# Four accumulating PSUM banks as four tensors of 512 columns instead of two of 1024, with a feature evicted in two halves

## The chip, the core and the metric

The kernel runs on one core of one Trainium2 chip. The metric is the device time of one execution in microseconds; the number given for a kernel is the median over its runs. In the profile, PE is the engine that multiplies matrices (PEld its weight loads, which run beside the multiplications), DVE the vector engine, ACT the scalar engine, POOL the general engine and SP the one that mostly issues transfers. Matmuls write to PSUM, a memory of eight banks here, each of which holds 512 fp32 columns on 128 partitions. A matmul of this kernel writes at most one bank; DVE and ACT read the finished sums from there ("evict" them) into SBUF.

## The reference

One layer of a conditioned decoder over 1024 positions and 1024 channels, in fp32. Cut to what matters:

```
mod = silu(c) @ ada_w + ada_b;  shift, scale, gate = split(mod, 3)
h = rms_norm(x, norm_w) * (1 + scale) + shift
hq, hf, hi, hz, gq, gk, gv, gz, ga, mg = split(h @ w_in)        # one wide projection
# hgrn: 8 heads of 128, gated linear recurrence
f = lb + (1 - lb) * sigmoid(hf);  k = (1 - lb) * sigmoid(-hf)
y_h = rms_norm(chunked_gated_linear_attention(silu(hq), k, hi, log f), hgrn_norm_w) * silu(hz)
# gla: 4 heads, key 128, value 256
log_a = log_sigmoid(ga @ alpha_w + alpha_b) / 16
y_g = rms_norm(chunked_gated_linear_attention(gq, gk, gv, log_a), gla_norm_w) * silu(gz)
merged = sigmoid(mg_0) * (y_h @ w_branch_0) + sigmoid(mg_1) * (y_g @ w_branch_1)
out = rms_norm(x + gate * (merged @ w_out), final_norm_w)
```

## The kernel before

Every large product is made of matmuls of 128 x 128 weights by 128 x 512 columns. To keep fp32 accuracy each operand is split into a high and a low part (ACT casts, L211 and its like; DVE subtracts, L212 and its like), and each product takes three matmuls.

The program has these stages. The **start** loads and normalises x and forms h. The **first group** (L386) makes six half rows of features in six accumulators `accs`: four PSUM banks and the two halves of `sc_ps`; DVE evicts them at L362 and L364 (`qk_out`). Then **V stage 0** (`Vstage`, matmuls at L1879, evictions at L1762, L1764, L1782, L1786 and L1790) makes values by a Strassen-like scheme: seven products in the order 1, 2, 5, 3, 6, 7, 4, each into the same four banks with 12 matmuls to a bank, six for one pair of operands and six for the next, and each bank evicted before the next product may start on it. The **features** (`mm_feat`, L594) are 34 blocks of 128 channels by 1024 positions, each 48 matmuls into two banks: 8 for silu(gz) and 24 for the hgrn part, of which 16 are evicted by a sigmoid on ACT (L949) and a product on DVE (L950), as the 8 of gz are too; 8 by two sigmoids (L1079, L1080); and two of gla_k by a DVE copy. V stage 1 stands among them. Beside them run twelve attention heads (L626 to L823), whose small matmuls (L652, L683, L741, L798, L817, L819) are slipped in between and write to `sc_ps` and to the `pm` tiles. The **last stages** (L1330) form the branch products and the gates in a ring of banks, four of which are the accumulating banks, lent at L1941, and the **out stage** (L1507) makes the output.

PSUM has three pools: `ps_d` holds the four accumulating banks as two tensors of 128 x 1024, two banks each (names pd...); `ps_s` holds one tensor `sc_ps` of two banks; `ps_m` two tensors of one bank (pm...). `dtile()` takes a tensor from `ps_d`; where single banks are wanted, the code cuts it in halves, so a matmul still writes one bank:

```
acc0 = [dtile(), dtile()]
accs = [acc0[f // 2][:, (f % 2) * 512:(f % 2) * 512 + 512] for f in range(4)]
```

Beyond the start, whose order is written out by hand, a scheduler decides at compile time which instruction stands where in each engine's queue, and which semaphores an instruction waits for. Evictions carry a raised priority. Each engine then runs its own queue in that fixed order.

Of the kernel before, what the change touches and what calls it, by code (L numbers as in the profile page):

```python
# [10 lines left out]
F32 = mybir.dt.float32  # L11
F32R = mybir.dt.float32r
I32 = mybir.dt.int32
AF = mybir.ActivationFunctionType
ALU = mybir.AluOpType

P = 128
D = 1024
T = 1024
# [70 lines left out]
def hybrid_trunk_kernel(  # L90
# [6 lines left out]
    nc = tc.nc  # L97
# [3 lines left out]
    cp = ctx.enter_context(tc.tile_pool(name="const", bufs=1))  # L101
    sp = ctx.enter_context(tc.tile_pool(name="slots", bufs=1))
    dp = ctx.enter_context(tc.tile_pool(name="dram", bufs=1, space=bass.MemoryType.DRAM))
    ps_d = ctx.enter_context(tc.tile_pool(name="ps_d", bufs=2, space=bass.MemoryType.PSUM))
    ps_s = ctx.enter_context(tc.tile_pool(name="ps_s", bufs=1, space=bass.MemoryType.PSUM))
    ps_m = ctx.enter_context(tc.tile_pool(name="ps_m", bufs=2, space=bass.MemoryType.PSUM))
    S = Slots(sp, N_SLOTS)
# [1 line left out]
    cnt = [0]  # L109

    def dtile():
        cnt[0] += 1
        return ps_d.tile([P, T], F32, tag="d", name=f"pd{cnt[0]}")

    def mtile():
        cnt[0] += 1
# [251 lines left out]
    def make_ga(half):  # L368
# [8 lines left out]
        if half == 0:  # L377
            S.free(*[hT[half, i] for i in range(4)])

    acc0 = [dtile(), dtile()]  # L380
    accs = [acc0[f // 2][:, (f % 2) * 512:(f % 2) * 512 + 512] for f in range(4)]
    accs += [sc_ps[:, 0:512], sc_ps[:, 512:1024]]

    def product(half, d, f, n):
# [202 lines left out]
    def mm_feat(wt, rhs, ps, w=P):  # L587
        hi, lo = wt
        for k in range(KT):
            n = 0  # L590
            r_hi, r_lo = rhs(k)
            for a, b in ((hi, r_hi), (hi, r_lo), (lo, r_hi)):
                for th in range(2):
                    nc.tensor.matmul(ps[0:w, th * 512:(th + 1) * 512], a[:, k, 0:w],  # L594
                                     b[:, th * 512:(th + 1) * 512],
                                     start=(k == 0 and n == 0), stop=(k == KT - 1 and n == 2))
                n += 1
            yield

    class Feat:  # L600
# [15 lines left out]
        def run(self):  # L616
            ps = dtile()
            yield from mm_feat(self.wt, self.rhs, ps, self.w)
            S.free(*self.wt)
            self.done(ps)  # L620
# [325 lines left out]
    def silu_done(store, key):  # L946
        def f(ps):
            s = S.get([T])
            nc.scalar.activation(s, ps, AF.Sigmoid)  # L949
            nc.vector.tensor_mul(s, s, ps)  # L950
            store[key] = s
        return f

# [59 lines left out]
    def gla_k_done(h):  # L1013
        def f(ps):
            t = S.get([T])
            nc.vector.tensor_copy(t, ps)
            if h == 3:
                nc.gpsimd.dma_start(k3_d, t)
                S.free(t, sent=True)
            else:  # L1020
                g_state[("k", h)] = t
        return f
# [53 lines left out]
    def hf_done(h):  # L1076
        def fn(ps):
            f, k = S.get([T]), S.get([T])
            nc.scalar.activation(f, ps, AF.Sigmoid)  # L1079
            nc.scalar.activation(k, ps, AF.Sigmoid, scale=-1.0)  # L1080
            nc.vector.tensor_scalar(f, f, oml[:, h:h + 1], lb[:, h:h + 1], ALU.mult, ALU.add)
            nc.vector.tensor_scalar_max(f, f, F_FLOOR)
            nc.vector.tensor_scalar_mul(k, k, oml[:, h:h + 1])
            h_state[("f", h)] = f
            h_state[("k", h)] = k
        return fn
# [205 lines left out]
    R = Banks()  # L1292
# [83 lines left out]
    def last_stages():  # L1376
        for n, (b, p) in enumerate(GROUPS):
            for i in range(4):
                if i % 2 == 0:
                    ahead(2 * n + i // 2, 4, 2)  # L1380
                pairs[b, i].run(p)
                pairs[b, i].after(p)
                for f in at.get((b, p, i), ()):
                    f()
            if b:
                for z in H.pop((0 if b == 1 else b, p)):
                    S.free(*z)
# [277 lines left out]
    for b in (2, 3):  # L1665
        for p, i, z in ((3, 3, "11"), (6, 1, "21"), (6, 3, "12"), (7, 2, "22")):
            after(b - 1, p, i, lambda b=b, z=z: load_quad(b, z))
            if b == 3:
                p, i = {(3, 3): (7, 2), (6, 1): (7, 3), (6, 3): (4, 2), (7, 2): (4, 3)}[p, i]
# [77 lines left out]
    class Vstage:  # L1747
# [5 lines left out]
            self.snap = {}  # L1753

        def start(self):
            pair = [dtile() for _ in range(2)]
            self.bank = [pair[i // 2][:, i % 2 * 512:i % 2 * 512 + 512] for i in range(4)]

        def take(self, i, scale=1.0):
            t = Q.get()  # L1760
# [178 lines left out]
    stream.go()  # L1939
    S.free(*h_hi, *h_lo)  # L1940
    lent = [dtile() for _ in range(2)]  # L1941
    R.lend([pd[:, i * 512:i * 512 + 512] for pd in lent[::-1] for i in range(2)])
    last_stages()
    out_stage()

# [28 lines left out]
```

## Time and profile before

| | |
|---|---|
| three runs | 1201.57, 1200.64, 1201.26 us; median 1201.26 |
| the profiled execution | 1201.55 us, of which the span of the trace is 1199.8 |
| PE matmuls | 1170.1 us busy, 98% of the span |
| DVE | 846.3 us busy, 71% |
| ACT | 584.9 us busy, 49% |
| POOL | 124.3 us busy, 10% |
| mean granted PE clock | 0.998 |

A matmul's busy time overlaps that of the one behind it, so that PE's busy share says how much of the span some matmul was in flight, not that it stepped at its full rate. The idle time before a group of instructions is listed with the instruction whose end let it go on ("<-", the releaser); it is the place to look for what a busy engine loses.

### The profile page before, as it was taken

The page shows a single profiled execution, that of the slowest core. Times are in us where ns is not written, and L with a number is a line of the kernel's source. Part 1 is how long each engine was busy: PE and PEld are TensorE (multiplying, and loading weights), DVE is VectorE, ACT ScalarE, POOL GpSimd, SP SyncE. Part 2 cuts the span into 40 slices and gives each one's busy share as a digit, 9 for nine tenths or more (in the row PEclk, how much of TensorE's full clock was granted, in tenths as well). Part 3 has the DMA queues.
Part 4 walks back from the last instruction along what each step waited for, and adds up shares of the span by engine and source line. Part 5 has one row for each costly group of instructions (what it writes and reads, how often), then busy time and mean ns, then how long its engine had stood idle before and what let it go on. Part 6 is the DMA issues. An engine that isn't in the chain of part 4 may idle for free.

```text
span 1199.8 us, 20303 instructions
## 1 busy us (share of the span) xinstructions
PE 1170.1 (98%) x8137; PEld 951.0 (79%) x8137; DVE 846.3 (71%) x1270; ACT 584.9 (49%) x860; POOL 124.3 (10%) x257
## 2 busy tenths in 40 slices
PE   7999999999999999999999999999999999999997
PEld 6776777888878688888888878778888888878886
DVE  4745667657664955887897798695553866988994
ACT  5674462673455445334433435456643644444554
POOL 4111111000110211111111010001120000000000
PEclk9999999999999999999999999999999999999999
DMA  9745445155474855665565454255688846335523
GB/s 324 262 173 201 150 161 176 52 178 175 167 273 141 296 195 161 209 210 160 173 197 178 130 203 124 78 169 179 225 312 284 285 152 210 125 108 173 171 99 134
DMA packets 150641, 221.24 MB, mean 184 GB/s; under 512 B 8971, under 2 KB 107329, under 8 KB 150546
## 3 DMA queue, kind: packets, MB, share of 16 engines
q1 hardware_dynamic: 132114, 158.37, 42.4%
q0 software_dynamic: 18384, 61.56, 13.3%
q8 instruction: 64, 1.05, 0.4%
q14 instruction: 31, 0.25, 0.1%
q10 hardware_dynamic: 48, 0.01, 0.0%
HBM read 154.37 MB, written 65.54 MB: 183 GB/s over the span
## 4 chain that ended last, share of the span: by engine, by line
PE 65%; issue 20%; DVE 6%; ACT 4%; DMA 3%; POOL 2%; SPq 0%; POOLq 0%; DVEq 0%; ACTq 0%
PE pd L594 16%; PE pd L1330 11%; PE pd L1879 9%; PE sc_ps L1330 6%; PE pm L1330 6%; PE pd L1507 3%; PE pd L386 2%; PE sc_ps L1507 2%; PE pm L1507 1%; PE pm L798 1%; POOL ws L1182 1%; DVE b L212 1%; PE pm L817 1%; DMA b<-in_ada_w_dram 1%; PE sc_ps L386 1%
## 5 line engine op out<-in xcount | busy, mean ns | idle before, releaser
L594 PE MATMUL pd<-b,b 128*128 128x512 f32 x1632 | 393.8, 396 | 0.2 <-ACT b L1762 0.2
L594 PEld LDWEIGHTS pd<-b,b 128*128 128x128 f32 x1632 | 303.0, 189 | 65.8 <-issue 0.7
L1330 PE MATMUL pd<-b,b 128*128 128x512 f32 x720 | 173.2, 392 | 0.6 <-DVE b L1422 0.4
L1879 PE MATMUL pd<-b,b 128*128 128x512 f32 x672 | 162.7, 396 | 7.1 <-DVE b L1790 3.4
L1330 PEld LDWEIGHTS pd<-b,b 128*128 128x128 f32 x720 | 133.9, 188 | 31.2 <-DVE b L1422 0.9
L1879 PEld LDWEIGHTS pd<-b,b 128*128 128x128 f32 x672 | 123.4, 188 | 40.7 <-ACT b L1762 4.0
L212 DVE TENSOR_TENSOR b<-b,b 128x1024 fp32r<-128x1024 f32 x78 | 94.2, 1222 | 48.4 <-ACT b L211 48.1
L1273 DVE TENSOR_TENSOR b<-b,b 128x1024 fp32r<-128x1024 f32 x56 | 68.2, 1221 | 69.2 <-ACT b L1272 53.0
L1272 ACT CAST b<-b 128x1024 fp32r<-128x1024 f32 x56 | 58.4, 1050 | 65.0 <-PE pm L1330 18.1
L211 ACT CAST b<-b 128x1024 fp32r<-128x1024 f32 x78 | 79.8, 1047 | 6.4 <-PE pd L1879 3.0
L1330 PE MATMUL sc_ps<-b,b 128*128 128x512 f32 x324 | 78.7, 391 | 0.4 <-ACT b L1302 0.4
L1330 PE MATMUL pm<-b,b 128*128 128x512 f32 x300 | 72.1, 389 | 0.0
L1330 PEld LDWEIGHTS sc_ps<-b,b 128*128 128x128 f32 x324 | 60.4, 188 | 13.9 <-ACT b L1302 1.1
L1249 ACT CAST b<-b 128x1024 fp32r<-128x1024 f32 x48 | 49.7, 1050 | 43.9 <-PE pd L1330 15.9
L1250 DVE TENSOR_TENSOR b<-b,b 128x1024 fp32r<-128x1024 f32 x48 | 57.7, 1219 | 18.4 <-ACT b L1249 12.2
L1330 PEld LDWEIGHTS pm<-b,b 128*128 128x128 f32 x300 | 56.3, 188 | 11.7
L203 DVE TENSOR_TENSOR b<-b,b 128x1024 fp32r<-128x1024 f32 (+1 forms) x36 | 35.1, 983 | 29.5 <-ACT b L202 29.4
L386 PE MATMUL pd<-b,b 128*128 128x512 f32 x192 | 52.3, 405 | 2.8 <-DVE b L362 1.9
L1182 POOL DMA_DIRECT2D ws<-b x64 | 34.9, 546 | 193.6 <-DVE b L1174 107.4
L703 ACT COPY xb<-b 128x512 f32<-128x512 f32 x48 | 29.7, 621 | 50.8 <-PE sc_ps L683 23.8
L817 PE MATMUL pm<-scT,b 128*128 128x128 f32 x256 | 46.9, 275 | 0.0
L386 PEld LDWEIGHTS pd<-b,b 128*128 128x128 f32 x192 | 34.4, 188 | 15.4 <-DVE b L362 2.9
(317 smaller groups left out, 1699.6 us busy)
## 6 DMA issues: line engine op xcount, KB each, us to landing
b<-in_w_in_dram SPq DMA_DIRECT2D x72, 512.0 KB, 4.3
ws<-b POOLq DMA_DIRECT2D x64, 256.0 KB, 3.9
b<-ws SPq DMA_DIRECT2D x32, 512.0 KB, 4.4
b<-in_x_dram SPq DMA_DIRECT2D x16, 512.0 KB, 4.4
b<-in_ada_w_dram SPq DMA_DIRECT2D x32, 256.0 KB, 6.5
v<-b POOLq DMA_DIRECT2D x32, 256.0 KB, 3.7
b<-v SPq DMA_DIRECT2D x16, 512.0 KB, 5.2
b<-fx SPq DMA_DIRECT2D x16, 512.0 KB, 4.5
```

What stands on the lines that cost most here:

```text
L211: held(nc.scalar.copy(hi, src))
L212: nc.vector.tensor_sub(lo, src, hi.bitcast(F32))
L386: nc.tensor.matmul(accs[f], wg(a, d, f), b[d][:, half * 512:half * 512 + 512], start=(d == 0 and n == 0), stop=(d == KT - 1 and n == 2))
L594: nc.tensor.matmul(ps[0:w, th * 512:(th + 1) * 512], a[:, k, 0:w], b[:, th * 512:(th + 1) * 512], start=(k == 0 and n == 0), stop=(k == KT ...
L817: nc.tensor.matmul(o, vch(ch)[:, vh * P:(vh + 1) * P], scT[:, ch, :], start=True, stop=(ch == 0))
L1249: nc.scalar.copy(hi, src)
L1250: nc.vector.tensor_sub(lo, src, hi.bitcast(F32))
L1272: nc.scalar.copy(hi, t)
L1273: nc.vector.tensor_sub(lo, t, hi.bitcast(F32))
L1330: nc.tensor.matmul(o, a[:, sl], c, start=(p in (1, 5) and kt == 0 and n == 0), stop=(kt == 3 and n == 2), skip_group_check=True)
L1507: nc.tensor.matmul(o, a, b, start=(p in (1, 5) and kt == 0 and n == 0), stop=(kt == 3 and n == 2), skip_group_check=True)
L1879: nc.tensor.matmul(st.bank[i], x_, w_, start=(p in (1, 5) and kk == 0 and a == 0 and n == 0), stop=(kk == 1 and a == 1 and n == 2), skip_g ...
```

## The change

`ps_d` now holds four tensors of 128 x 512, one bank each, and `dtile()` returns a list of two of them. The banks, and which matmul adds to which sum, are the same as before; `accs`, the banks of `Vstage` and those lent to the last stages are now four tensors. An instruction that reads or writes 1024 columns of a feature at once can no longer do so, since they lie in two tensors: the sigmoid and product of `silu_done`, the two sigmoids of `hf_done` and the copy of `gla_k_done` are each done for 512 columns and then for the other 512.

```diff
-    ps_d = ctx.enter_context(tc.tile_pool(name="ps_d", bufs=2, space=bass.MemoryType.PSUM))
+    ps_d = ctx.enter_context(tc.tile_pool(name="ps_d", bufs=4, space=bass.MemoryType.PSUM))
...
     def dtile():
         cnt[0] += 1
-        return ps_d.tile([P, T], F32, tag="d", name=f"pd{cnt[0]}")
+        return [ps_d.tile([P, 512], F32, tag="d", name=f"pd{cnt[0]}_{i}") for i in range(2)]
...
-    acc0 = [dtile(), dtile()]
-    accs = [acc0[f // 2][:, (f % 2) * 512:(f % 2) * 512 + 512] for f in range(4)]
+    accs = dtile() + dtile()
     accs += [sc_ps[:, 0:512], sc_ps[:, 512:1024]]
...
                 for th in range(2):
-                    nc.tensor.matmul(ps[0:w, th * 512:(th + 1) * 512], a[:, k, 0:w],
+                    nc.tensor.matmul(ps[th][0:w, :], a[:, k, 0:w],
...
     def silu_done(store, key):
         def f(ps):
             s = S.get([T])
-            nc.scalar.activation(s, ps, AF.Sigmoid)
-            nc.vector.tensor_mul(s, s, ps)
+            for th in range(2):
+                sl = slice(th * 512, th * 512 + 512)
+                nc.scalar.activation(s[:, sl], ps[th], AF.Sigmoid)
+                nc.vector.tensor_mul(s[:, sl], s[:, sl], ps[th])
             store[key] = s
...
             t = S.get([T])
-            nc.vector.tensor_copy(t, ps)
+            for th in range(2):
+                nc.vector.tensor_copy(t[:, th * 512:th * 512 + 512], ps[th])
...
             f, k = S.get([T]), S.get([T])
-            nc.scalar.activation(f, ps, AF.Sigmoid)
-            nc.scalar.activation(k, ps, AF.Sigmoid, scale=-1.0)
+            for th in range(2):
+                sl = slice(th * 512, th * 512 + 512)
+                nc.scalar.activation(f[:, sl], ps[th], AF.Sigmoid)
+                nc.scalar.activation(k[:, sl], ps[th], AF.Sigmoid, scale=-1.0)
...
         def start(self):
-            pair = [dtile() for _ in range(2)]
-            self.bank = [pair[i // 2][:, i % 2 * 512:i % 2 * 512 + 512] for i in range(4)]
+            self.bank = dtile() + dtile()
...
     lent = [dtile() for _ in range(2)]
-    R.lend([pd[:, i * 512:i * 512 + 512] for pd in lent[::-1] for i in range(2)])
+    R.lend([pd for pds in lent[::-1] for pd in pds])
```

The scheduler puts instructions in another order on PE and DVE. Line numbers behind the first edit shift by up to four: L386 becomes L385, L645 becomes L644, L1790 becomes L1793, L1879 becomes L1882.

PE at the end of the first group, before: the three matmuls that finish the first half of `sc_ps`, then three that finish the second bank of pd_173. The first banks of pd_173 and pd_174 are finished ahead of these rows.

```order
L386 MATMUL sc_ps<-b_146,b_168 128x512
L386 MATMUL sc_ps<-b_154,b_168 128x512
L386 MATMUL sc_ps<-b_146,b_170 128x512
L386 MATMUL pd_173<-b_146,b_162 128x512
L386 MATMUL pd_173<-b_154,b_162 128x512
L386 MATMUL pd_173<-b_146,b_166 128x512
```

The same place in the changed kernel (pd_1_176 is the fourth bank, pd_0_1139 and pd_1_1140 the first two of V stage 0, which take the room of the first two accumulators).

```order
L385 MATMUL pd_1_176<-b_154,b_162 128x512
L385 MATMUL pd_1_176<-b_146,b_166 128x512
L385 MATMUL sc_ps<-b_146,b_168 128x512
L385 MATMUL sc_ps<-b_154,b_168 128x512
L385 MATMUL sc_ps<-b_146,b_170 128x512
L1882 MATMUL pd_0_1139<-b_1078,b_139 128x512
L1882 MATMUL pd_0_1139<-b_1079,b_139 128x512
L1882 MATMUL pd_0_1139<-b_1078,b_147 128x512
L1882 MATMUL pd_0_1139<-b_1078,b_140 128x512
L1882 MATMUL pd_0_1139<-b_1079,b_140 128x512
L1882 MATMUL pd_0_1139<-b_1078,b_148 128x512
L1882 MATMUL pd_1_1140<-b_1078,b_139 128x512
```

All four banks are now finished in the order first, second, third, fourth ahead of the first half of `sc_ps`, and V stage 0 begins straight behind it; before, six matmuls of the group (banks two and four) stood behind that place.

PE in V stage 0 at the end of product 7, before: the last three of five matmuls into the third bank (in pd_1138), and then the first three of the six into the second bank, which lies in pd_1137; the six into the first bank, in pd_1137 too, stand ahead of all of these. b_1499 and b_1500 are the weights, b_1505 and b_1506 the columns.

```order
L1879 MATMUL pd_1138<-b_1499,b_1506 128x512
L1879 MATMUL pd_1138<-b_1499,b_1505 128x512
L1879 MATMUL pd_1138<-b_1500,b_1505 128x512
L1879 MATMUL pd_1137<-b_1499,b_1505 128x512
L1879 MATMUL pd_1137<-b_1500,b_1505 128x512
L1879 MATMUL pd_1137<-b_1499,b_1506 128x512
```

The same place in the changed kernel: the last two of the first bank and the first three of the second.

```order
L1882 MATMUL pd_0_1139<-b_1504,b_1509 128x512
L1882 MATMUL pd_0_1139<-b_1503,b_1510 128x512
L1882 MATMUL pd_1_1140<-b_1503,b_1509 128x512
L1882 MATMUL pd_1_1140<-b_1504,b_1509 128x512
L1882 MATMUL pd_1_1140<-b_1503,b_1510 128x512
```

Behind these rows stand three more of the second bank, six matmuls of pd_0_1141 and six of pd_1_1142, and only then the first of product 4 on pd_0_1139; before, product 4's first three on the first bank stood ahead of product 7's six on the fourth. The second bank now follows the first without a piece of the third between them, and so it is through both V stages: six matmuls to each bank in turn.

DVE at the evictions of product 7 (L1790), beside the preparation of a head (L645 to L648, L654 to L657) and a split (L212), before:

```order
L212 TENSOR_TENSOR b_1586<-b_1318,b_1585 128x1024
L1790 TENSOR_TENSOR b_1327<-pd_1137,b_1327 128x512
L645 TENSOR_TENSOR xb<-b_1519,b_863 128x32x8
L646 TENSOR_TENSOR xb<-b_1519,b_863 128x32x8x2
L212 TENSOR_TENSOR b_1623<-b_1517,b_1622 128x1024
L1790 TENSOR_TENSOR b_1327<-pd_1137,b_1327 128x512
L1790 TENSOR_TENSOR b_1350<-pd_1138,b_1350 128x512
L647 TENSOR_TENSOR xb<-xb,b_863 128x32x16
```

The same place in the changed kernel:

```order
L212 TENSOR_TENSOR b_1590<-b_1322,b_1589 128x1024
L1793 TENSOR_TENSOR b_1331<-pd_0_1139,b_1331 128x512
L1793 TENSOR_TENSOR b_1331<-pd_1_1140,b_1331 128x512
L644 TENSOR_TENSOR xb<-b_1523,b_865 128x32x8
L645 TENSOR_TENSOR xb<-b_1523,b_865 128x32x8x2
L1793 TENSOR_TENSOR b_1354<-pd_0_1141,b_1354 128x512
L646 TENSOR_TENSOR xb<-xb,b_865 128x32x16
L1793 TENSOR_TENSOR b_1354<-pd_1_1142,b_1354 128x512
L647 TENSOR_TENSOR xb<-xb,b_865 128x32x8
L212 TENSOR_TENSOR b_1627<-b_1521,b_1626 128x1024
```

The second bank's eviction now stands directly behind the first one's, and the split that stood between them (b_1623 before, b_1627 now) has moved behind all four.

## The prediction

> **What bounds the kernel now.** I read the page's first and fifth parts first: how busy each engine is, and which groups of instructions have idle time before them.
>
> ```profile
> span 1199.8 us, 20303 instructions
> ...
> PE 1170.1 (98%) x8137; PEld 951.0 (79%) x8137; DVE 846.3 (71%) x1270; ACT 584.9 (49%) x860; POOL 124.3 (10%) x257
> ...
> L594 PE MATMUL pd<-b,b 128*128 128x512 f32 x1632 | 393.8, 396 | 0.2 <-ACT b L1762 0.2
> ...
> L1330 PE MATMUL pd<-b,b 128*128 128x512 f32 x720 | 173.2, 392 | 0.6 <-DVE b L1422 0.4
> L1879 PE MATMUL pd<-b,b 128*128 128x512 f32 x672 | 162.7, 396 | 7.1 <-DVE b L1790 3.4
> ...
> L386 PE MATMUL pd<-b,b 128*128 128x512 f32 x192 | 52.3, 405 | 2.8 <-DVE b L362 1.9
> ```
>
> PE is the bound: 98% of the span. The change neither adds nor takes away a matmul, so it can only gain what PE loses between matmuls, and that is small in the features (L594: 0.2 us) and sits in the V stages (L1879: 7.1 us) and the first group (L386: 2.8 us). The rate of an unbroken run is in the chain of work that ended last:
>
> ```profile
> 467.08 21.76 PE pd L594 x96
> ```
>
> 96 matmuls in 21.76 us are 0.2267 us each, however long one is in flight. Next, PE's waits by releaser:
>
> ```profile
> PE pd L1879 <- DVE b L1790: 3.4, 3, 1.6
> ...
> PE pd L386 <- DVE b L362: 1.9, 1, 1.9
> PE sc_ps L652 <- DVE xb L648: 1.9, 1, 1.9
> PE sc_ps L683 <- DVE blk L666: 1.3, 1, 1.3
> PE pd L1879 <- ACT b L1762: 1.3, 4, 0.7
> ...
> PE pd L1879 <- DVE b L212: 0.6, 1, 0.6
> ...
> PE pd L1879 <- ACT b L211: 0.6, 1, 0.6
> ...
> PE pd L1879 <- DVE b L362: 0.5, 2, 0.3
> PE pd L1330 <- DVE b L1422: 0.4, 1, 0.4
> ...
> PE pd L1879 <- DVE b L1786: 0.3, 1, 0.3
> PE pd L1879 <- ACT b L1764: 0.2, 1, 0.2
> ...
> PE pd L1330 <- ACT b L1401: 0.2, 1, 0.2
> ```
>
> The columns are us in total, times, and the longest. The releasers L1790, L1762, L1764, L1786, L362, L1422 and L1401 are all evictions of the accumulating banks, 8.2 us together. Whether PE had to wait for them is the question. The timeline around the end of V stage 0's product 7 answers it:
>
> ```profile
> 175.70 3.33 PE L1879 MATMUL pd<-b,b 128*128 128x512 f32 x14
> ...
> 179.85 0.68 DVE L1790 TENSOR_TENSOR b<-pd,b 128x512 f32<-128x512 f32 x1
> 180.45 0.64 DVE L645 TENSOR_TENSOR xb<-b,b 128x256 f32<-128x256 f32 x1
> 180.59 1.89 PE L1879 MATMUL pd<-b,b 128*128 128x512 f32 x7 [1.55 <-DVE b L1790]
> ...
> 180.97 0.85 DVE L646 TENSOR_TENSOR xb<-b,b 128x512 f32<-128x512 f32 x1
> 181.69 1.21 DVE L212 TENSOR_TENSOR b<-b,b 128x1024 fp32r<-128x1024 f32 x1
> 182.81 1.28 DVE L1790 TENSOR_TENSOR b<-pd,b 128x512 f32<-128x512 f32 x2
> ...
> 183.65 5.69 PE L1879 MATMUL pd<-b,b 128*128 128x512 f32 x24 [1.17 <-DVE b L1790]
> ```
>
> By the order before, the matmuls that begin at 180.59 are product 7's own into the second bank, and the first L1790 (179.85) evicts product 7's first bank. The two share nothing but the tensor pd_1137. So a matmul into one bank of a tensor waits until the other bank has been read: a false wait, put there because waits are kept per tensor. The wait at 183.65 is product 4's first bank, which needs the first L1790, done at 180.53, but waits for the second one, done about 183.5.
>
> **The change part by part.** *False waits in V stage 0.* With a tensor to a bank the scheduler gives each bank six matmuls in turn; product 4's first on a bank comes 18 matmuls, 18 x 0.2267 = 4.1 us, behind product 7's last on it. An eviction of 0.68 us has 3.4 us of room. What the stage loses now, I take from a window of it:
>
> ```profile
> 116.39:180.59 64.20, 61.68 (x262) 48.35 (x262) 43.80 (x41) 32.20 (x41) 8.81 (x17) 1.00 0.46 163
> ...
> 704.00:712.00 8.00, 7.36 (x84) 6.00 (x85) 8.00 (x15) 1.95 (x3) 0.00 (x0) 0.79 0.56 192
> ```
>
> The columns are the window and its length, busy us and count for PE, PEld, DVE, ACT and POOL, then the granted clock. In 64.20 us PE issued 262 matmuls, worth 262 x 0.2267 = 59.40: 4.8 us lost, of which the wait table names about 2.5 (1.55 at its end, and 0.2 to 0.3 each for L1764, L1786 and two of L1762). The other 2.3 us over five stalls, 0.4 to 0.5 each, are draining and restarting, which the idle column does not show. From 180.59 to 183.65 seven matmuls took 3.06 us instead of 1.59: 1.5 us more. Together 6.3 us, all of which goes if the evictions keep their room. At the last of these the new DVE order puts both first L1790s back to back: by before's rows the first ends at 180.53. The first bank's last matmul is in the piece of 14 that ends at 179.03, five from its end, so at about 177.9, and product 4 follows 4.1 us behind it, at 182.0: no wait, by 1.4 us. **6.3 us.**
>
> *First group.* The timeline:
>
> ```profile
> 106.87 1.23 DVE L909 TENSOR_TENSOR b<-b,b 128x1024 f32<-128x1024 f32 x1 [3.65 <-ACT b L907]
> 107.13 0.84 PE L386 MATMUL sc_ps<-b,b 128*128 128x512 f32 x3
> ...
> 108.02 1.22 DVE L212 TENSOR_TENSOR b<-b,b 128x1024 fp32r<-128x1024 f32 x1
> ...
> 109.15 0.68 DVE L362 TENSOR_SCALAR b<-pd 128x512 f32<-128x512 f32 x1
> ...
> 109.89 0.53 PEld L386 LDWEIGHTS pd<-b,b 128*128 128x128 f32 x3 [2.34 <-DVE b L362]
> 109.89 0.96 PE L386 MATMUL pd<-b,b 128*128 128x512 f32 x3 [1.92 <-DVE b L362]
> ```
>
> The second accumulator waits 1.92 us for the eviction of the first, which is late behind L909 and an L212. In the new order six matmuls (the second and fourth banks) come ahead of the first that needs this eviction, V stage 0's: 6 x 0.2267 = 1.4 us of the wait are filled, and about 0.6 stay, a true wait now. The two later L362 waits (0.5 us with their restarts about 1.3) go in part: the second half of sc_ps, which stays one tensor, still waits for the first half's eviction. I take 0.4. **1.8 us**, between 1.0 and 3.2.
>
> *V stage 1 and the last stages.* L1790's third wait (3.4 - 1.55 - 1.17 = 0.7) and L1762's longest (0.7) lie in V stage 1; each with a restart of 0.4, that is 2.2 us. L1422 and L1401 with restarts: 0.4 + 0.2 + 0.8 = 1.4 us. **3.6 us.** The waits for splits (L211, L212: 0.6 each) are for operands and stay.
>
> *Evictions in halves.* The groups of ACT and DVE:
>
> ```profile
> L949 ACT ACTIVATE b<-pd 128x1024 f32<-128x1024 f32 x24 | 24.6, 1027 | 38.7 <-PE pd L594 37.6 <-issue 1.1
> L1762 ACT COPY b<-pd 128x512 f32<-128x512 f32 x32 | 18.3, 588 | 39.1 <-PE pd L1879 38.9
> ```
> ```profile
> L950 DVE TENSOR_TENSOR b<-b,pd 128x1024 f32<-128x1024 f32 x24 | 29.8, 1241 | 20.7 <-ACT b L949 20.6
> ```
>
> Two of 588 ns for one of 1027: 0.15 us more for each of 24 sigmoids and of hf's 16: 40 x 0.15 = 6 us on ACT. On DVE two of 0.68 (L1790's) for one of 1.241: 0.12 us for each of 24 products, and I take as much for the two copies: 3 us. Queue by queue: on DVE the second product now waits for the second sigmoid, and behind it stands a head's preparation (L645 to L666), which PE's L652 or L683 waits for. Of hf, f is whole after three of four half sigmoids, 3 x 0.588 = 1.76, instead of after one of 1.027, so DVE's next step (L1081) comes 0.7 us later, eight times. What hides all this: a feature is 48 matmuls, 10.9 us, ACT sat idle 38.7 us before L949 for want of PE, and the features' matmuls need only the banks back. If this cover were gone everywhere, the price would be 6 + 3 + 8 x 0.7 = 15 us; at the other end, a bank that comes free after its own half could take away the L594 wait of 0.2. I take **0**, nearest to that 0.2.
>
> *What comes late next.* PE arrives earlier, by 8 us from 185 us on, at waits that others set: those for L211 and L212, and for L648 and L666 in two heads. The producers are themselves paced by features and buffers that PE frees, so they move along in the main, but transfers do not. I take **2 us** back; between 0 and all of the gain.
>
> Sum: 6.3 + 1.8 + 3.6 - 0 - 2 = 9.7 us. From the profiled execution's 1201.55 that is 1191.85; this execution was 0.3 above the median of 1201.26, so I write **1191.5 us**, 0.8% less. What a measurement here can tell from no change is about 0.2%, 2.4 us.
>
> **The rivals.** *The gain is absorbed.* A wait that DVE or a transfer times does not move with PE. For it: DVE is busy in all of the 8 us from 704 to 712, and one head there waits 1.9 us for L648; if DVE's queue in the features were the second bound, PE would gain 8 us and wait them off there. Against it: over the span DVE is idle 29%, and of the waits shown only two lie at heads. Time: 1201.5 minus only the 3.6 - 2.2 = 1.4 us behind the features and perhaps 3 in all: 1197 to 1200.
>
> *Slower: a head gets late and the clock falls.* This is the place:
>
> ```profile
> 704.64 1.31 PE L652 MATMUL sc_ps<-xb,b 128*32 128x80 f32 x64 [1.89 <-DVE xb L648]
> 705.88 6.45 PE L594 MATMUL pd<-b,b 128*128 128x512 f32 x20
> ```
>
> After that wait, 20 matmuls took 6.45 us instead of 20 x 0.2267 + 0.16 = 4.7, and the window's granted clock is 0.79: the late head cost 1.9 and another 1.75, so 3.7 us. If a half eviction (0.68 us, with its wait for the second sigmoid up to 0.6 more) is put ahead of L648 or L666 where a head has no slack, a head is late by 1.3 more, and the same falls to others. The sign turns at three more such heads of twelve, 11.1 us against a gain of 9.7: 1202.9; four give 1206.6. For it: two heads are late by over a microsecond already. Against it: ten are not.
>
> *Banks in turn as a clock problem.* The granted clock was 1.00 in the window of V stage 0, with stalls of 0.2 to 1.6 us between banks. The mechanism would be that going round the banks every six matmuls leaves small gaps that lower the clock; at half of it for the same 262 matmuls alone the stage would take 59 us more, 1250 us in all. The Trainium skill ("TensorE: Matmul & The Clock Gate", section "A second HAM failure mode: psum-queue depth-cycling") says that a kernel cycling through PSUM banks had its PE pause so often between groups that the clock went up and down. The trace speaks against that here: gaps between the same four banks exist before, and the clock stays.
>
> *It does not do what it says.* If the framework still held back a bank for its neighbour (a pool's release, say), nothing would go: 1201 to 1202. The new order, with six matmuls to a bank in turn, speaks against it, since the scheduler would have interleaved them again.
>
> **How the numbers follow.** Forecast, a gain of 7 to 13 us: 0.66. More than that (the L666 wait and the clock's 1.75 go as well, 1186.5): 0.05. Absorbed: 0.15, a third of it within 2.4 us. Not done: 0.03. Late heads: 0.10, one part in ten of it within 2.4 us. Clock: 0.01. Faster by over 0.2%: 0.66 + 0.05 + 0.10 = 0.81; the same: 0.05 + 0.03 + 0.01 = 0.09; slower: 0.10. The range from 1186.5 to 1199 leaves out the cases without gain and the slow ones, 0.2.
>
> **What would show it.** Right: no wait of L1882 for an eviction (L1793, L1765, L1789) above 0.3 us; from the first to the last product the V stage at 0.227 us a matmul; a remaining wait of 0.5 to 0.8 us at V stage 0's first matmul for the first accumulator; ACT some 6 and DVE some 3 us busier; L594 still without idle time. Wrong: waits of L652 or L683 that grew by as much as the V stages lost (absorbed), more stretches with a granted clock under 1.00 in the features (late heads), or L1882 waits of the same size (not done).

## The result, and the profile after

| | before | changed |
|---|---|---|
| median of 5 runs | 1201.26 us (1199.9 to 1201.57) | 1189.22 us (1185.92 to 1189.62) |
| ratio, 95% interval | | 0.9895 [0.9881, 0.991] |
| profiled execution; its span | 1201.55; 1199.8 us | 1185.92; 1184.2 us |

The change takes 12 us, 1%, off the median. The profiled execution of the changed kernel was the shortest of its five, so the two traces differ by 15.6 us; what is in that difference beside the change is told below.

The page of the changed kernel, engines and costliest groups, to be set beside the rows of before:

```profile
span 1184.2 us, 20359 instructions
...
PE 1159.0 (98%) x8137; PEld 951.7 (80%) x8137; DVE 847.0 (72%) x1296; ACT 587.2 (50%) x900; POOL 123.9 (10%) x257
...
L593 PE MATMUL pd<-b,b 128*128 128x512 f32 x1632 | 392.0, 396 | 0.8 <-DVE b L212 0.8
L1334 PE MATMUL pd<-b,b 128*128 128x512 f32 x720 | 170.4, 390 | 0.0
L1882 PE MATMUL pd<-b,b 128*128 128x512 f32 x672 | 157.4, 392 | 2.6 <-ACT b L211 1.3
```

PE has the same 8137 matmuls. The V stages' idle time (L1882) fell from 7.1 to 2.6 us, and no eviction is its main releaser any more. ACT has 40 more activations and DVE 26 more instructions, for 2.3 and 0.7 us of busy time.

PE's waits in the changed kernel, by releaser (us in total, times, longest):

```profile
...
PE sc_ps L651 <- DVE xb L647: 1.8, 1, 1.8
PE pd L1882 <- ACT b L211: 1.3, 1, 1.3
PE sc_ps L385 <- DVE b L364: 1.3, 1, 1.3
PE pm L816 <- DVE b L803: 0.9, 1, 0.9
PE pd L593 <- DVE b L212: 0.8, 1, 0.8
...
PE pd L1882 <- DVE b L362: 0.7, 1, 0.7
PE pd L1882 <- DVE b L212: 0.6, 1, 0.6
PE sc_ps L1334 <- DVE b L1426: 0.6, 1, 0.6
PE sc_ps L1334 <- ACT b L1306: 0.4, 1, 0.4
PE sc_ps L1511 <- ACT b L1565: 0.4, 1, 0.4
```

Of the waits for evictions of the accumulating banks (8.2 us before), one of 0.7 us is left: V stage 0's first matmul, which really needs the first accumulator's bank. Four more waits for evictions (L364, L1426, L1306, L1565) are on `sc_ps`, which is still one tensor of two banks. V stage 0 in the changed kernel's timeline is now one piece:

```profile
113.13 67.99 PE L1882 MATMUL pd<-b,b 128*128 128x512 f32 x299
181.04 1.31 PE L651 MATMUL sc_ps<-xb,b 128*32 128x80 f32 x64
```

299 matmuls from 113.13 to the next piece at 181.04 are 0.2271 us each, close to the 0.2267 of an unbroken run. The evictions of product 7 stand close together in DVE's queue, and PE does not see them:

```profile
175.43 1.28 DVE L1793 TENSOR_TENSOR b<-pd,b 128x512 f32<-128x512 f32 x2
...
177.87 0.67 DVE L1793 TENSOR_TENSOR b<-pd,b 128x512 f32<-128x512 f32 x1
...
179.22 0.69 DVE L1793 TENSOR_TENSOR b<-pd,b 128x512 f32<-128x512 f32 x1
```

### The profile page after: what moved, and what is told of

Read it like the earlier page. It is cut to its first block, busy times and chain, and to the rows that moved or that the text cites. A ratio compares the mean times of both kernels' runs of the same rounds, so it can differ in the third digit from the quotient of the medians.

```text
span 1184.2 us, 20359 instructions
## 1 busy us (share of the span) xinstructions
PE 1159.0 (98%) x8137; PEld 951.7 (80%) x8137; DVE 847.0 (72%) x1296; ACT 587.2 (50%) x900; POOL 123.9 (10%) x257
## 3 DMA queue, kind: packets, MB, share of 16 engines
q0 software_dynamic: 18384, 61.56, 13.5%
## 4 chain that ended last, share of the span: by engine, by line
PE 61%; issue 20%; DVE 8%; ACT 4%; DMA 4%; POOL 2%; SPq 0%; POOLq 0%; DVEq 0%; ACTq 0%
PE pd L593 14%; PE pd L1882 11%; PE pd L1334 10%; PE sc_ps L1334 5%; PE pm L1334 4%; PE pd L1511 3%; PE pd L385 2%; PE sc_ps L1511 2%; PE pm L1511 1%; POOL ws L1186 1%; DMA b<-in_ada_w_dram 1%; PE sc_ps L385 1%; PE pm L816 1%; PE pm L797 1%; PE pm L818 1%
## 5 line engine op out<-in xcount | busy, mean ns | idle before, releaser
L593 PE MATMUL pd<-b,b 128*128 128x512 f32 x1632 | 392.0, 396 | 0.8 <-DVE b L212 0.8
L1334 PE MATMUL pd<-b,b 128*128 128x512 f32 x720 | 170.4, 390 | 0.0
L1882 PE MATMUL pd<-b,b 128*128 128x512 f32 x672 | 157.4, 392 | 2.6 <-ACT b L211 1.3
L1882 PEld LDWEIGHTS pd<-b,b 128*128 128x128 f32 x672 | 125.3, 188 | 30.1 <-ACT b L211 1.7
L212 DVE TENSOR_TENSOR b<-b,b 128x1024 fp32r<-128x1024 f32 x78 | 94.5, 1224 | 43.9 <-ACT b L211 43.6
L1334 PEld LDWEIGHTS pm<-b,b 128*128 128x128 f32 x300 | 56.3, 188 | 11.7
L385 PE MATMUL pd<-b,b 128*128 128x512 f32 x192 | 51.6, 403 | 0.9 <-ACT b L202 0.8
L816 PE MATMUL pm<-scT,b 128*128 128x128 f32 x256 | 46.9, 275 | 0.9 <-DVE b L803 0.9
L385 PEld LDWEIGHTS pd<-b,b 128*128 128x128 f32 x192 | 34.6, 188 | 12.7 <-issue 1.7
```

The costliest lines, as they stand in the source:

```text
L212: nc.vector.tensor_sub(lo, src, hi.bitcast(F32))
L385: nc.tensor.matmul(accs[f], wg(a, d, f), b[d][:, half * 512:half * 512 + 512], start=(d == 0 and n == 0), stop=(d == KT - 1 and n == 2))
L593: nc.tensor.matmul(ps[th][0:w, :], a[:, k, 0:w], b[:, th * 512:(th + 1) * 512], start=(k == 0 and n == 0), stop=(k == KT - 1 and n == 2))
L816: nc.tensor.matmul(o, vch(ch)[:, vh * P:(vh + 1) * P], scT[:, ch, :], start=True, stop=(ch == 0))
L1334: nc.tensor.matmul(o, a[:, sl], c, start=(p in (1, 5) and kt == 0 and n == 0), stop=(kt == 3 and n == 2), skip_group_check=True)
L1882: nc.tensor.matmul(st.bank[i], x_, w_, start=(p in (1, 5) and kk == 0 and a == 0 and n == 0), stop=(kk == 1 and a == 1 and n == 2), skip_g ...
```

## The experiments

My theory: waits are kept per tensor, so that two banks in one tensor hold up each other; a tensor to a bank takes these waits away, in the V stages above all, and the halved evictions are hidden. The rivals: the gain comes from the halved evictions (a bank is free sooner); or it comes from the features, by a stretch of low clock and a late head that happen to be missing in the new trace. Medians, with the runs of before that shared the chip:

| run | what | median (range), us | before | ratio, 95% interval |
|---|---|---|---|---|
| e0_again | the changed kernel | 1187.53 (1186.36 to 1189.14) | 1201.23 | 0.9889 [0.9875, 0.9902] |
| e1_halves | halves alone | 1202.49 (1200.76 to 1203.62) | 1201.23 | 1.0009 [1.0, 1.0017] |
| e2_pair | other pairs of banks | 1195.36 (1194.51 to 1195.91) | 1201.23 | 0.9952 [0.994, 0.9965] |
| e3_first | four tensors up to V stage 0 | 1192.25 (1191.42 to 1193.18) | 1201.23 | 0.9929 [0.9916, 0.9943] |
| e4_sc | `sc_ps` split too | 1185.58 (1182.8 to 1187.07) | 1201.54 | 0.9862 [0.9847, 0.9878] |
| e5_quarters | evictions in quarters | 1188.45 (1186.5 to 1193.03) | 1201.54 | 0.9896 [0.9879, 0.9913] |
| e6_later | four tensors from the features on | 1195.72 (1194.15 to 1201.5) | 1201.54 | 0.9956 [0.9944, 0.9968] |
| e7_after | the changed kernel | 1189.25 (1187.72 to 1191.49) | 1202.76 | 0.9893 [0.9873, 0.9912] |
| e8_sc | e4_sc again | 1185.62 (1184.41 to 1187.82) | 1202.76 | 0.9862 [0.984, 0.9884] |

**e0_again.** No edit.

> The changed kernel once more. Its five runs lay between 1185.92 and 1189.62 us, and the profiled one was the fastest, so the trace shows 15.6 us less than before while the medians differ by 12.0. If a stretch at half clock, which cost about 1.75 us before and is missing in that trace, comes and goes between executions, this profile is nearer 1189 and shows a granted clock under 1.00 somewhere in the features. If the spread is in the start, the features look as they did and PE's times up to 60 us differ. Either way 1186 to 1190.

1187.53 us; the profiled execution took 1187.9. Its clock was lower over a short stretch, but in V stage 1 and not in the features. Windows of its trace (length, busy us and counts of PE, PEld, DVE, ACT, POOL, then granted clock, DMA share and GB/s) and the piece ahead:

```profile
392.00:396.00 4.00, 3.36 (x11) 2.61 (x11) 4.00 (x6) 3.05 (x4) 1.61 (x3) 0.70 0.90 249
396.00:400.00 4.00, 4.00 (x17) 3.27 (x16) 2.59 (x6) 0.00 (x0) 1.08 (x2) 0.87 1.00 326
```
```profile
391.20 0.81 PE L1882 MATMUL pd<-b,b 128*128 128x512 f32 x2 [1.04 <-ACT b L211]
392.65 8.95 PE L1882 MATMUL pd<-b,b 128*128 128x512 f32 x31 [0.64 <-DVE b L212]
```

So the stretch moves: the head that it followed before (L652 at 704.64, here L651 at 695.66) has a clock of 1.00 here, and in the other trace of the same kernel it is missing at both places. The 31 matmuls of the second row take 8.95 us here and 7.33 us in that other trace, so a part of the spread between executions is this, some 1.6 us.

**e1_halves.** On the kernel before:

```diff
-            nc.scalar.activation(s, ps, AF.Sigmoid)
-            nc.vector.tensor_mul(s, s, ps)
+            for th in range(2):
+                sl = slice(th * 512, th * 512 + 512)
+                nc.scalar.activation(s[:, sl], ps[:, sl], AF.Sigmoid)
+                nc.vector.tensor_mul(s[:, sl], s[:, sl], ps[:, sl])
```

and so for the sigmoids of hf and the copies of gla_k.

> Two tensors of 1024 as before, only the evictions of the features in halves. Theory (a wait is kept per tensor, and the new tensors take the false ones away): the V stages keep their waits (L1790 3 to 3.5 us, L1762 about 1.3), the halves are hidden, 1199.5 to 1202. Rival (the gain comes from the halves, which free banks and start DVE earlier): 1189 to 1195. If the halves cost what their engines do more and it is not hidden: 1203 to 1210.

1202.49 us, a little above what I expected, and no gain at all. Its waits:

```profile
PE pd L1885 <- DVE b L1796: 3.5, 3, 1.7
...
PE pd L386 <- DVE b L362: 1.9, 1, 1.9
...
PE pd L1885 <- ACT b L1768: 1.3, 4, 0.7
```

The false waits of V stage and first group stand as before (L1796 and L1768 are L1790 and L1762). The rival "halves" falls for halves in a shared tensor. Since a wait is for the whole tensor, a half eviction frees no bank there; for halves beside tensors of their own bank the next but one experiment, e3_first, is the better evidence: it has no halves at all. What the halves do here shows in ACT's groups:

```profile
L951 ACT ACTIVATE b<-pd 128x512 f32<-128x512 f32 x48 | 28.7, 598 | 65.9 <-DVE b L952 32.8 <-PE pd L594 31.8 <-issue 1.1
```

ACT's second sigmoid waits for DVE's first product (L952, 32.8 us in all, in 20 of the 24 features), though of PSUM the two only read, and different banks of the same tensor. They also work on the two halves of one SBUF tensor, `s`. In the changed kernel `s` is still one tensor and only the banks have a tensor each, and there the wait is gone: the group's idle time is PE's.

```profile
L950 ACT ACTIVATE b<-pd 128x512 f32<-128x512 f32 x48 | 26.2, 596 | 29.9 <-PE pd L593 29.0 <-ACT xb L676 0.8
```

**e2_pair.** On the kernel before, one line, in the V stages alone:

```diff
-            self.bank = [pair[i // 2][:, i % 2 * 512:i % 2 * 512 + 512] for i in range(4)]
+            self.bank = [pair[i % 2][:, i // 2 * 512:i // 2 * 512 + 512] for i in range(4)]
```

> Before, with one line changed: in the V stages a tensor holds banks 1 and 3 or banks 2 and 4 of a product instead of 1 and 2 or 3 and 4. Nothing is smaller, nothing is halved. Theory: the false wait is now for a bank that was finished six matmuls (1.4 us) earlier, so the short stalls for ACT's evictions (0.6 to 1.1 us with their restarts) go, while those for DVE's late L1790 stay in part: 1195 to 1199. Rival (the size of the tensors or the halves matter, not who shares a tensor): 1200 to 1202.

1195.36 us, 5.9 less. Nothing is smaller and nothing halved; only which two banks share a tensor is another. Its waits for L1790 are shorter, and no matmul of L1879 waits for L1762 any more (a head's L683 has a new wait for it, 0.8 us); the first group, which was not changed, keeps its wait:

```profile
PE pd L386 <- DVE b L362: 1.9, 1, 1.9
...
PE pd L1879 <- DVE b L1790: 1.5, 3, 0.7
```

That settles that the waits are the tensors' and not the banks', and it fits that their cost depends on how long ago the neighbour was finished. The instructions' order follows the tensors too, here as in the changed kernel; no run holds the order and changes the tensors alone, so what the waits and what the order give is not separated.

**e3_first and e6_later.** e3_first is the kernel before with a pool of four tensors for `accs` and V stage 0, closed behind it, and the old pool of two opened then; e6_later is the changed kernel with a pool of two tensors of 1024 at that place and the four behind it. The core of e3_first:

```diff
     def dtile():
         cnt[0] += 1
-        return ps_d.tile([P, T], F32, tag="d", name=f"pd{cnt[0]}")
+        if not ps_2:
+            ps_4.__exit__(None, None, None)
+            ps_2.append(ctx.enter_context(tc.tile_pool(name="ps_d", bufs=2, space=bass.MemoryType.PSUM)))
+        return ps_2[0].tile([P, T], F32, tag="d", name=f"pd{cnt[0]}")
...
-    accs = [acc0[f // 2][:, (f % 2) * 512:(f % 2) * 512 + 512] for f in range(4)]
+    accs = four()
```

> Four tensors of 512 only for the first group and V stage 0; then the pool is closed and everything else is as before, whole evictions too. Theory: the first head's L652 comes 8 to 9 us earlier than before, V stage 1 keeps its waits for L1790 and L1762 (2.2 us with restarts), head 11 and the last stages theirs: 1191 to 1194. Rival (most of the gain is in the features, the clock and the heads): 1197 to 1201.

> The complement of e3_first: two tensors of 1024 for the first group and V stage 0, then four of 512 with halved evictions for all that follows. e3_first took 9.0 of the change's 12 to 13.7 us. Theory (places add up): V stage 0 keeps its L1790 and L362 waits; V stage 1, head 11 and the last stages gain 2.7, 1.9 and 0.8 by the lead of PE in the two traces: 1195.5 to 1198.5. Rival (an early lead feeds later gains, or the later ones are chance): 1199 to 1202.

1192.25 us, 9.0 less than before, and 1195.72 us, 5.8 less. Together 14.8; the whole change gave 12.0, 13.7 and 13.5 in three comparisons. The places add up to 1 to 3 us more than the whole, about the spread of a kernel's runs (e6_later's reach from 1194.15 to 1201.5), the first group and V stage 0 being the larger part. e3_first has that part with whole evictions, so it needs no halves. e6_later has tensors and halves together, and its 5.8 us are not split between them. In its trace both waits are back, with the low clock behind each of them; in the trace of before the clock is 1.00 at these places:

```profile
108.00:112.00 4.00, 2.67 (x8) 1.82 (x9) 2.96 (x5) 3.55 (x5) 1.63 (x3) 0.82 0.29 113
112.00:116.00 4.00, 4.00 (x14) 3.14 (x14) 3.18 (x5) 0.00 (x0) 1.61 (x3) 0.75 0.48 182
180.00:184.00 4.00, 2.58 (x7) 1.53 (x7) 4.00 (x6) 0.17 (x1) 0.54 (x1) 0.78 0.66 182
184.00:188.00 4.00, 3.62 (x13) 3.01 (x14) 3.86 (x8) 0.00 (x0) 1.08 (x2) 0.79 0.84 277
```
```profile
109.33 0.96 PE L395 MATMUL pd<-b,b 128*128 128x512 f32 x3 [1.92 <-DVE b L372]
...
181.32 2.58 PE L1892 MATMUL pd<-b,b 128*128 128x512 f32 x7 [1.88 <-DVE b L1803]
```

**e4_sc and e8_sc.** The changed kernel, with `sc_ps` as two tensors of 512 in the first group and again in the last and out stages. In between, where the heads' reads cross both banks, it is one of 1024; one matmul of 128 columns is added to clear what the heads read without having written it. The edit at the last stages:

```diff
-        R.lend([sc_ps[:, 0:512], sc_ps[:, 512:1024]])
+        sc_open.pop().__exit__(None, None, None)
+        sc_open.append(tc.tile_pool(name="ps_c", bufs=2, space=bass.MemoryType.PSUM))
+        last_pool = sc_open[0].__enter__()
+        R.lend([last_pool.tile([P, 512], F32, tag="s", name=f"sb{i}") for i in range(2)])
```

> The changed kernel with the same done to sc_ps where single banks of it are used: two tensors of 512 in the first group and in the last and out stages, one of 1024 for the heads in between (its pool is closed and opened anew, and one matmul of 128 columns clears what the heads read without writing). Theory: the waits that remain on a neighbour bank of sc_ps (L385 for L364 1.3 us, L1334 for L1426 0.6 and L1306 0.4, L1511 for L1565 0.4) go with a restart of some 0.2 each: 3 to 4 us less than the changed kernel's 1187.5 to 1189.2, so 1184 to 1186. Rival (what waited there waits for the next thing): 1187 to 1189.5.

> The changed kernel beside e8_sc on one chip, for that comparison: 1186 to 1190, as in its two runs so far.

> e4_sc again, beside the changed kernel. Its trace showed the waits of the last and out stages for neighbour banks of sc_ps gone (1.4 us with no restart counted), and of the first group's 0.7 + 1.3 us a single wait of 1.3 left. If that is what it is worth, the median is 2 to 3 us under e7_after's; if e4_sc's 1185.6 was the spread of the start, the two lie within 1 us.

1185.58 us, and 1185.62 against 1189.25 for the changed kernel on the same chip: 3.6 us less there, more than the 2 to 3 that I expected, with four runs each whose ranges just meet. It beats both kernels. The waits of e4_sc for L1426, L1306 and L1565 are gone; in the first group the two waits of 0.7 and 1.3 us gave way to one:

```profile
PE pd L1887 <- DVE b L364: 1.3, 1, 1.3
```

L364 of this kernel is L362. The wait is no longer one of V stage 0's first matmul: the last six matmuls on `sc_ps`'s two tensors now fill that one. It stands behind V stage 0's first twelve matmuls, at the first on the third bank, for the eviction of the third accumulator:

```profile
110.27 3.00 PE L1887 MATMUL pd<-b,b 128*128 128x512 f32 x12
114.58 5.74 PE L1887 MATMUL pd<-b,b 128*128 128x512 f32 x24 [1.31 <-DVE b L364]
```

In that place the rival (what waited there waits for the next thing) was right for 1.3 of the 2.0 us.

**e5_quarters.** The changed kernel with the sigmoids and products in four pieces of 256:

```diff
-            for th in range(2):
-                sl = slice(th * 512, th * 512 + 512)
-                nc.scalar.activation(s[:, sl], ps[th], AF.Sigmoid)
-                nc.vector.tensor_mul(s[:, sl], s[:, sl], ps[th])
+            for qt in range(4):
+                sl, pq = slice(qt * 256, qt * 256 + 256), ps[qt // 2][:, qt % 2 * 256:qt % 2 * 256 + 256]
+                nc.scalar.activation(s[:, sl], pq, AF.Sigmoid)
+                nc.vector.tensor_mul(s[:, sl], s[:, sl], pq)
```

and so for the two sigmoids of hf; the copies of gla_k stay in halves.

> The changed kernel with the features' sigmoids and products in four pieces of 256 instead of two of 512: the cost of splitting evictions once more and doubled. By 0.40 us for 256 columns on ACT (0.59 for 512) and 0.42 on DVE (0.68), ACT has 80 x 0.2 = 16 us more and DVE 48 x 0.16 = 8 us. Theory (hidden): 1187 to 1190.5. If the cover is thin, heads get late: L651 and L682 wait longer, 1191 to 1197.

1188.45 us, inside the range of the changed kernel: the cost of splitting is hidden once more when doubled, in the median; one of its runs took 1193.03. Its sigmoids show a wait for DVE's product of the same total as in e1_halves, now between two quarters of one bank's tensor. Here the two share the bank as well as the tensor, so this run does not tell which of them it is:

```profile
L950 ACT ACTIVATE b<-pd 128x256 f32<-128x256 f32 x96 | 33.4, 384 | 60.2 <-DVE b L951 32.8 <-PE pd L593 26.4 <-ACT xb L676 0.8
```

## Why the prediction was right, step by step

The prediction was 1191.5 us in a range from 1186.5 to 1199; 1189.22 came. The range held, and so did the cause; inside the sum several terms were mis-sized, some too small and some too large. I compare the steps by PE's lead, the time by which the same matmuls come earlier in the trace of the changed kernel. Rows of before:

```profile
105.77 1.52 PE L386 MATMUL pd<-b,b 128*128 128x512 f32 x6
...
207.51 0.67 PE L741 MATMUL sc_ps<-xb 128*16 128x16 f32 x62
...
319.69 1.52 PE L1879 MATMUL pd<-b,b 128*128 128x512 f32 x6
...
488.77 1.31 PE L652 MATMUL sc_ps<-xb,b 128*32 128x80 f32 x64
...
814.02 0.67 PE L741 MATMUL sc_ps<-xb 128*16 128x16 f32 x62
...
1190.33 2.88 PE L1507 MATMUL pd<-b,b 128*128 128x512 f32 x12
```

and of the changed kernel:

```profile
105.00 2.88 PE L385 MATMUL pd<-b,b 128*128 128x512 f32 x12
...
109.21 1.86 PE L1882 MATMUL pd<-b,b 128*128 128x512 f32 x7 [0.65 <-DVE b L362]
...
198.51 0.67 PE L740 MATMUL sc_ps<-xb 128*16 128x16 f32 x62
...
311.51 1.52 PE L1882 MATMUL pd<-b,b 128*128 128x512 f32 x6
...
477.04 1.31 PE L651 MATMUL sc_ps<-xb,b 128*32 128x80 f32 x64
...
799.14 0.67 PE L740 MATMUL sc_ps<-xb 128*16 128x16 f32 x62
...
1174.70 2.88 PE L1511 MATMUL pd<-b,b 128*128 128x512 f32 x12
```

The lead is 0.8 us near the first group's end, ahead of its waits (the start, which the change doesn't touch), 9.0 at the first head's L741, 8.2 at V stage 1's first matmul, 11.7 at the fifth head, 14.9 at the last head's L741 and 15.6 at the end.

- **First group and V stage 0:** forecast 1.8 + 6.3 = 8.1; the lead grows by 8.2, and e3_first alone gave 9.0 in the median. The mechanism and its sum were right; the split between the two was less so. From 105.77 to 116.39 before, 31 matmuls took 10.62 us, 3.6 more than 31 x 0.2267; from 105.00 to 113.13 now, 25 take 8.13, 2.5 more. The first group gained 1.1 and not 1.8: the second half of `sc_ps` now waits 1.3 us for the first half's eviction, for which my sum had left 0.9 us with the restart. The wait for the first accumulator was forecast at 0.6 and is 0.65. Up to product 4 V stage 0 gained 6.2, as forecast; another 0.9 lies behind that, around the wait for L1762 at 197.04 (0.18 us), which I had left out.
- **V stage 1:** forecast 2.2. From its first matmul to the fifth head the lead grows by 3.5, although the stage's wait for a split became 0.7 longer, so the term was too small. The two waits that I had counted gave about 0.9 each; the rest comes up where heads' matmuls stand in other pieces between the stage's own, and nothing here separates it.
- **Last stages:** forecast 1.4; 0.7. The two stalls that I had counted went, but two waits for evictions of `sc_ps` (0.6 for L1426, 0.4 for L1565) are new, which e4_sc takes away. That for L1306 (0.4) is as old as the kernel before, where it stands as L1302.
- **Evictions in halves, 0:** right in the trace: ACT and DVE are 2.3 and 0.7 us busier (I had worked out 6 and 3), two sigmoids of 596 ns for one of 1027, two products of 697 for one of 1241. Neighbours overlap a little, and busy time counts that once: 48 sigmoids of 596 ns are 28.6 us in sum, but 26.2 of busy time. And e5_quarters doubles it without a cost in the median. e1_halves at [1.0, 1.0017] allows a cost of up to 2 us where both halves lie in one tensor.
- **What comes late next, 2 us back:** this came, at 2.4 us. A head's L816 waits 0.86 us for DVE, which takes the lead from 9.0 to 8.2 ahead of V stage 1; the split's wait in V stage 1 grew from 0.61 to 1.31; a feature now waits 0.84 for L212. Rows of the changed kernel:

```profile
293.75 0.71 PE L816 MATMUL pm<-scT,b 128*128 128x128 f32 x4 [0.86 <-DVE b L803]
...
389.67 0.81 PE L1882 MATMUL pd<-b,b 128*128 128x512 f32 x2 [1.31 <-ACT b L211]
...
709.84 2.11 PE L593 MATMUL pd<-b,b 128*128 128x512 f32 x8 [0.84 <-DVE b L212]
```

- **What the sum did not have:** between the fifth and the last head the lead still grew by 3.2 us. The low clock of 706 us is missing in this trace (the 24 matmuls behind that head take 5.77 us instead of 7.35, so 1.6 us and not the 1.75 that I had read), and the last head's L683, which waited 1.3 us for L666, does not wait at all, worth 1.9 us of lead. The forecast gave both together a chance of one in twenty. The last head's place in the changed kernel:

```profile
784.41 4.24 PE L1334 MATMUL pd<-b,b 128*128 128x512 f32 x18
788.58 0.89 PE L682 MATMUL sc_ps<-xb,b 128*32 128x48 f32 x64
```

Before, 12 matmuls of L1330 stood at that place and the wait behind them; the scheduler has now put 18 there, and six matmuls, 1.4 us, fill the wait; that it could because the banks are free apart is likely, not shown. In e3_first, where the features and last stages have the old tensors, 12 stand there and the wait is still there (L691 and L674 are L683 and L666):

```profile
PE sc_ps L691 <- DVE blk L674: 1.3, 1, 1.3
```

The rivals: *absorbed* falls, of the 9.0 us won by the first head the waits above take back 2.4. *Late heads* falls by its own sign: the late head's L651 waits 1.8 us, 1.9 before. The new wait of L816 (0.86 us, 1.6 in e0_again) needs no halves: e2_pair, with whole evictions, has it too (1.3 us). *Banks in turn* falls: V stage 0 runs at a clock of 1.00 in the traces of the changed kernel, six matmuls to a bank in turn, and the low clock of e0_again in V stage 1 stands behind waits for splits. *It does not do what it says* falls, since no wait of L1882 for L1793, L1765 or L1789 is listed.

The median gained 12.0 to 13.7 us where the traces differ by 15.6: 0.8 of that is the start, and some 1.6 the low clock, neither of which belongs to every execution. The forecast was 9.7. Most of what it lacked are the last head's 1.9 us and what V stage 1 gave beyond 2.2, neither of which it had in its sum; smaller gains than forecast in the first group and the last stages set some of that off, which is luck.

## What to carry to other kernels

Look at what shares a tensor before looking at what shares a bank: where PE waits for an eviction, ask whether it is the eviction of the bank it writes, and if not, give each bank a tensor of its own, or at least pair it with the bank that was finished longest ago. A stall's price is not its idle column alone: here five stalls of V stage 0 before the change, with 2.5 us of idle time, cost 4.8 us. And a wait that stays on the path grows when PE arrives earlier, so take its new size, not the old one.

## What I had not expected

- Two engines that only read one PSUM tensor are kept apart too: ACT's sigmoid of one half waited for DVE's product of the other, 32.8 us over 24 features in e1_halves; with a tensor to each bank the wait is gone.
- The low clock comes behind waits of PE of one to two microseconds, in some executions and not in others: 0.70 behind waits of 1.04 and 0.64 us at 391 us in e0_again, 0.82 and 0.78 around waits of 1.92 and 1.88 us in e6_later, none of it at the 1.8 us wait of the changed kernel's first trace, at its 1.31 us wait of 389.67, or at the 1.92 us wait of before. So the length of the wait alone does not decide it; what does was not tried. It makes single traces differ by one or two microseconds beside what a change itself is worth.
